# One more small read at the start of a kernel whose time is its transfers: 256 bytes of each partition's first row of strip 0, on ScalarE's DMA queue

## The chip, the cores and the metric

One core of one Trainium2 chip. HBM is the memory in which the input lies. A transfer (DMA) is issued by one of the compute engines on its queue and is carried out in packets by 16 transfer engines, which the text calls engines where packets are spoken of. The metric is the time of one execution on the device in microseconds (us), as the median of several runs; the span in a profile is the time from the first to the last instruction, and is some 1.7 us shorter. Ratios are the mean time of one kernel's fast runs over that of the other's of the same rounds, so not quite the ratio of the medians that are quoted.

## The reference

Four matrices of 4224 x 4224 fp32 numbers are summed up along both axes; of each result the diagonal is taken, and that is summed up once more.

```python
def reference(x):                       # x: (4, 4224, 4224) float32
    ps = np.cumsum(np.cumsum(x, axis=1), axis=2)
    diag = np.diagonal(ps, axis1=1, axis2=2)
    return np.cumsum(diag, axis=1).astype(np.float32)
```

Every number of the input counts, so 4 x 4224 x 4224 x 4 bytes = 285.5 MB have to be read once.

## The kernel before

The input is read in strips of 768 rows. A strip has 6 rows on each of the 128 partitions and is narrowed to bf16 by the load, which GpSimd issues. Three buffers hold strips. `head`, a corner of the last batch, stays fp32 and is loaded first, by SyncE; VectorE uses it at about 20 us.

```python
    head = last.tile([P, F, HC], FP32, name="head")            # P = 128, F = 3, HC = 384
    nc.sync.dma_start(out=head, in_=src[:, :, NH:N])
    # [cut: strip_tile]
    def load_rows(o, b, r0):
        f = o.shape[1]
        nc.gpsimd.dma_start(
            out=o, in_=x[b, r0 : r0 + f * P, :].rearrange("(p f) w -> p f w", f=f)
        )

    prefetched = []
    for i in range(NBUF):                                      # NBUF = 3
        t = strip_tile()
        load_rows(t, 0, i * F2 * P)                            # F2 = 6
        prefetched.append(t)
    # [cut: constants and masks]
    # for each strip, inside add_up:
            nc.vector.tensor_mul(out=mu, in0=block, in1=um)    # the diagonal block's masked part
            nc.vector.tensor_sub(out=block, in0=block, in1=mu)
            # [cut: TensorE sums columns; ScalarE (act_sum) and VectorE (row_sums) sum rows]
```

## Time and profile before

| | before |
|---|---|
| time, median of the first 3 runs | 667.07 us (667.06 to 667.53) |
| span of the profiled run | 665.4 us |
| read from HBM | 285.47 MB |
| first strip landed | 34.61 us |
| last load landed | 662.31 us |
| work after it | 3.1 us |

The page's tenths, queues, chain, waits and first windows are shown and read in the prediction. Besides these views I use the records of single DMA packets that the trace holds: start, duration, bytes and queue of each. Three rows of a strip arrive as one packet of 25,344 bytes written (50,688 read), which takes 1,886 ns; 16 of them on each of 16 engines are a strip, about 29.9 us. The records don't name the engine; where an engine is spoken of, I chained each packet to the one that ended just before it.

### The profile page before, as it was taken

Reading aid. Unit: us, or ns where it says so; the run is one execution under the profiler, and the core shown is the slowest. Engines: PE = TensorE matmul, PEld = TensorE weight load, DVE = VectorE, ACT = ScalarE, POOL = GpSimd, SP = SyncE. Lnnn points to the kernel's source line nnn. Section 1 sums busy time; section 2 is a strip of 40 time slices with the busy share of each in tenths; the row PEclk is TensorE's granted clock in tenths of the full one; section 3 lists DMA queues with packets and bytes.
Section 4 is the critical chain, followed back from the end, with each engine's and each line's share of the span. In section 5 each row is a group of like instructions: output and inputs, shape, how many; then the busy total and the mean of one; then the engine's idle time right before and its main releaser. Section 6 shows DMA issues by size and latency. Waiting matters only on the chain.

```text
span 665.4 us, 2461 instructions
## 1 busy us (share of the span) xinstructions
PE 201.7 (30%) x948; PEld 103.7 (16%) x948; DVE 326.4 (49%) x136; ACT 136.9 (21%) x222; POOL 31.8 (5%) x62
## 2 busy tenths in 40 slices
PE   0081423402007143140200623404032163250418
PEld 0040211201004021120100312202011031120103
DVE  3261625456906153454780524436388243352767
ACT  0001121406300103040630020304063002030434
POOL 6100000000000000000000000000000000001000
PEclk9995857656558585666755957666565586766758
DMA  9999999999999999999999999999999999999998
GB/s 206 219 219 219 219 219 215 212 210 218 219 218 219 219 220 218 218 213 212 216 218 218 217 219 219 218 219 211 215 216 219 219 214 220 216 219 216 214 208 162
DMA packets 7631, 143.25 MB, mean 215 GB/s; under 512 B 536, under 2 KB 1604, under 8 KB 2116
## 3 DMA queue, kind: packets, MB, share of 16 engines
q0 software_dynamic: 7152, 142.44, 99.9%
q1 hardware_dynamic: 468, 0.66, 0.3%
q8 instruction: 7, 0.11, 0.1%
q14 instruction: 4, 0.03, 0.0%
HBM read 285.47 MB, written 0.07 MB: 429 GB/s over the span
## 4 chain that ended last, share of the span: by engine, by line
another core or an unknown queue 44%; DVE 42%; DMA 11%; issue 1%; POOL 0%; PE 0%; DVEq 0%; POOLq 0%
DVE acc L246 27%; DMA strip<-in_x_dram 11%; DVE mu L333 7%; DVE strip L334 7%; DVE c L440 0%; POOL strip L411 0%; DVE rows L348 0%; PE d L226 0%; POOL strip L400 0%; DVE pu L246 0%; PE fin_e L226 0%; DVE c L266 0%; DVE pair L255 0%; PE carry_ps L226 0%
## 5 line engine op out<-in xcount | busy, mean ns | idle before, releaser
L226 PE MATMUL d<-strip,sel 128*33 128x384 bf16 (+1 forms) x603 | 140.7, 408 | 397.9 <-DMA strip<-in_x_dram 397.9
L241 ACT ACTIVATE dump<-strip 128x416 bf16<-128x416 bf16 (+6 forms) x110 | 125.1, 1138 | 520.5 <-DMA strip<-in_x_dram 517.8
L333 DVE TENSOR_TENSOR mu<-strip,um 128x4608 bf16<-128x4608 bf16 (+1 forms) x24 | 52.4, 2183 | 316.4 <-DMA strip<-in_x_dram 316.3
L246 DVE TENSOR_REDUCE acc<-strip 128x6 f32<-128x4608 bf16 (+6 forms) x23 | 196.0, 8523 | 0.8
L226 PEld LDWEIGHTS <-sel 128*33 128x33 bf16 (+1 forms) x849 | 94.9, 112 | 534.1 <-issue 495.9
L226 PE MATMUL d<-mu,sel 128*33 128x384 bf16 (+1 forms) x243 | 48.9, 353 | 45.4 <-DVE mu L333 45.4
L334 DVE TENSOR_TENSOR strip<-strip,mu 128x4608 bf16<-128x4608 bf16 (+1 forms) x24 | 52.4, 2183 | 1.0
L80 POOL DMA_DIRECT2D strip<-in_x_dram x24 | 16.5, 687 | 536.7 <-DVE acc L246 312.3
L241 ACT ACTIVATION_READ_ACCUMULATOR dump<-strip 128x1 f32 x110 | 20.5, 186 | 0.0
L226 PE MATMUL fold<-strip,ident_h 128*128 128x480 bf16 x8 | 3.4, 601 | 10.8 <-DMA strip<-in_x_dram 10.8
L96 DVE MEMSET um<- 128x6144 bf16 x1 | 5.2, 5178 | 1.2 <-issue 1.2
L216 DVE TENSOR_SCALAR steps<-steps 128x128 int32<-128x128 int32 x1 | 0.2, 227 | 11.0 <-POOL steps L215 11.0
L101 POOL TENSOR_SCALAR_AFFINE_SELECT um<-um 128x4608 bf16<-128x4608 bf16 (+1 forms) x2 | 5.2, 2614 | 4.0 <-DVE um L96 4.0
L226 PEld LDWEIGHTS <-ident_h 128*128 128x128 bf16 x21 | 2.2, 113 | 14.8 <-issue 13.8
L411 POOL DMA_DIRECT2D strip<-in_x_dram x5 | 2.7, 552 | 26.5 <-DMA strip<-in_x_dram 26.5
L226 PE MATMUL d<-ones_all,rows 128*33 128x128 f32 (+1 forms) x12 | 2.3, 347 | 5.4 <-DVE rows L348 5.4
L226 PE MATMUL fold_a<-strip,ident_h 128*128 128x512 bf16 x13 | 3.3, 380 | 0.3 <-DMA strip<-in_x_dram 0.3
L246 DVE TENSOR_REDUCE parts<-strip 128x3 f32<-128x3072 bf16 x1 | 3.4, 3352 | 0.0
L400 POOL DMA_DIRECT2D strip<-in_x_dram x2 | 1.4, 714 | 30.8 <-DVE acc L246 30.8
L226 PEld LDWEIGHTS d<-halves,rows 128*33 128x33 f32 (+1 forms) x24 | 2.5, 150 | 0.7 <-issue 0.5
L226 PE MATMUL d<-halves,rows 128*33 128x64 f32 (+1 forms) x24 | 2.6, 284 | 0.0
L348 DVE TENSOR_TENSOR rows<-acc 64x30 f32<-64x30 f32 (+2 forms) x12 | 2.1, 177 | 0.9
(80 smaller groups left out, 34.7 us busy)
## 6 DMA issues: line engine op xcount, KB each, us to landing
strip<-in_x_dram POOLq DMA_DIRECT2D x19, 6336.0 KB, 76.6
strip<-in_x_dram POOLq DMA_DIRECT2D x5, 3168.0 KB, 59.8
strip<-in_x_dram POOLq DMA_DIRECT2D x1, 1152.0 KB, 50.2
strip<-in_x_dram POOLq DMA_DIRECT2D x1, 768.0 KB, 53.3
strip<-in_x_dram POOLq DMA_DIRECT2D x3, 240.0 KB, 54.3
head<-in_x_dram SPq DMA_DIRECT2D x1, 576.0 KB, 4.0
strip<-in_x_dram POOLq DMA_DIRECT2D x1, 176.0 KB, 43.2
strip<-in_x_dram POOLq DMA_DIRECT2D x1, 64.0 KB, 28.6
```

What stands on the lines that cost most here:

```text
L80: nc.gpsimd.dma_start(out=o, in_=x[b, r0 : r0 + f * P, :].rearrange("(p f) w -> p f w", f=f))
L96: nc.vector.memset(um_all, 1.0)
L101: nc.gpsimd.affine_select(out=um, in_=um, compare_op=ALU.is_gt, fill=0.0, base=0, pattern=[[-1, f], [1, f * P]], channel_multiplier=-f,)
L216: nc.vector.tensor_single_scalar(out=steps, in_=steps, scalar=2, op=ALU.arith_shift_right)
L226: nc.tensor.matmul(o, lhsT=lhsT, rhs=rhs, start=start, stop=False, skip_group_check=True)
L241: nc.scalar.activation(out=dump[:, :w], in_=src, func=ACT.Copy, accum_out=acc)
L246: nc.vector.reduce_sum(out=acc, in_=src, axis=AX.X)
L333: nc.vector.tensor_mul(out=mu, in0=block, in1=um)
L334: nc.vector.tensor_sub(out=block, in0=block, in1=mu)
L348: nc.vector.tensor_add(out=o, in0=acc[..., 0], in1=acc[..., 1])
L400: nc.gpsimd.dma_start(out=part_a[:, :, c0:c1], in_=src_a[:, :, c0:c1])
L411: nc.gpsimd.dma_start(out=part_b[:, sb, c0:c1], in_=x[b, r0 : r0 + R, :NH].rearrange("r (k c) -> r k c", k=4)[:, :, c0:c1],)
```

## The change

ScalarE issues a read of 128 x 256 bytes, the first 64 numbers of each partition's first row of strip 0, into a tile that nothing uses. Its intent, as the words of it have it, is to touch that memory while the first load runs.

```diff
     head = last.tile([P, F, HC], FP32, name="head")
     nc.sync.dma_start(out=head, in_=src[:, :, NH:N])
+
+    touch = last.tile([P, 64], FP32, name="touch")
+    nc.scalar.dma_start(
+        out=touch, in_=x[0, : F2 * P, :].rearrange("(p f) w -> p f w", f=F2)[:, 0, :64]
+    )
```

## The prediction

> **What bounds the kernel now.** I read four views of the kernel before, in this order: the page (its tenths, DMA queues and HBM line), the chain that ended last, the waits, and the windows of the first microseconds.
>
> The page first, its engines, tenths, queues and bytes:
>
> ```profile
> PE 201.7 (30%) x948; PEld 103.7 (16%) x948; DVE 326.4 (49%) x136; ACT 136.9 (21%) x222; POOL 31.8 (5%) x62
> ...
> DMA  9999999999999999999999999999999999999998
> GB/s 206 219 219 219 219 219 215 212 210 218 219 218 219 219 220 218 218 213 212 216 218 218 217 219 219 218 219 211 215 216 219 219 214 220 216 219 216 214 208 162
> DMA packets 7631, 143.25 MB, mean 215 GB/s; under 512 B 536, under 2 KB 1604, under 8 KB 2116
> ## 3 DMA queue, kind: packets, MB, share of 16 engines
> q0 software_dynamic: 7152, 142.44, 99.9%
> q1 hardware_dynamic: 468, 0.66, 0.3%
> ...
> HBM read 285.47 MB, written 0.07 MB: 429 GB/s over the span
> ```
>
> No compute engine is busy for half of the span; the DMA engines are busy in every one of the 40 slices. The queue that GpSimd fills (q0, the strip loads, which narrow fp32 to bf16 on the way) alone accounts for 99.9% of the 16 engines' time. The bytes moved are counted as written (bf16), so 219 GB/s written stands for twice as much read: the HBM line gives 429 GB/s over the whole span, start and tail included.
>
> Next the chain that ended last, three pieces of it in order of time (start us, us, what):
>
> ```profile
> 1.33 33.28 DMA strip<-in_x_dram
> ...
> 619.08 43.23 DMA strip<-in_x_dram
> 662.33 0.40 DVE pair L255 x2
> ```
>
> The chain begins with the first strip's load, from 1.33 to 34.61 us, and its last load lands at 619.08 + 43.23 = 662.31 us; behind it there are only 665.4 - 662.3 = 3.1 us of work. In between the chain alternates between VectorE and pieces named "another core or an unknown queue" (44% on the page); those are the load waits once more, as the waits show:
>
> ```profile
> ACT dump L241 <- DMA strip<-in_x_dram: 517.8, 23, 62.4
> ...
> PE d L226 <- DMA strip<-in_x_dram: 397.9, 20, 34.7
> DVE mu L333 <- DMA strip<-in_x_dram: 316.3, 20, 19.8
> POOL strip L80 <- DVE acc L246: 312.3, 10, 32.2
> ```
>
> Every engine waits for strips, ScalarE longest: 62.4 us at one go, at the start. GpSimd in turn waits for a free buffer, but since three strips are in the buffers and two are queued while one is summed, the DMA tenths show no hole from that. So the end is set by the transfer engines' total work. Last, the windows of the start (columns: window, length, busy time of PE, PEld, DVE, ACT and POOL with counts, TensorE clock, DMA share, GB/s):
>
> ```profile
> 1.00:2.00 1.00, 0.00 (x0) 0.10 (x1) 0.08 (x2) 1.00 (x1) 0.67 (x1) 1.00 0.04 12
> 2.00:2.50 0.50, 0.00 (x0) 0.00 (x0) 0.13 (x1) 0.10 (x1) 0.50 (x2) 1.00 1.04 157
> 2.50:3.00 0.50, 0.00 (x0) 0.00 (x0) 0.50 (x1) 0.00 (x0) 0.50 (x2) 1.00 0.51 126
> ```
>
> The first packets run at about 1.9 us; until the strips begin at 3.8 to 4.5 us (the packet records, engine by engine) only the `head` tile that SyncE's queue reads is moving, and it doesn't fill the engines (0.51 between 2.5 and 3.0 us). Packets are entered at their starts in these short windows, so only the low shares mean something.
>
> **What the Trainium skill says.** Three places on its page "DMA: Bandwidth & Descriptors". Section "Issuing engines are not separate DMA queues": a DMA issued by ScalarE, SyncE or GpSimd ends up on the same 16 DMA engines and interleaves there. So the new read isn't free for being on ScalarE's queue. The trace agrees in kind: while the first result is stored, at 521 us, one 1,536-byte packet of SyncE's queue goes between two strip packets of an engine, and the spacing of those packets is 1,940 ns where strip packets alone follow each other every 1,866 ns. Section "Specifications": a fabric ceiling of 435 GB/s, and 512 bytes as the least transfer for line rate. For the ceiling the trace agrees: 285.47 MB between the first strip packet (3.8 us) and the last landing (662.3 us) is 433.5 GB/s. Whether a 256-byte packet costs more than its share is not shown before the change. Section "Why small descriptors are slow (HBM only)": a fixed overhead of about 3 cycles a packet, 11 cycles for 256 bytes where 8 carry data. The trace has nothing of that size that reads HBM; it has packets close by, used below.
>
> **The change part by part.** Nothing is removed, and nothing is moved: set side by side, the instruction lists of GpSimd, TensorE, VectorE and SyncE are the same up to buffer numbers and the number of the semaphore that `head` reports on. ScalarE gets one instruction more, a DMA issue ahead of its table load. Nothing reads the new tile, so no instruction waits for it.
>
> Step 1, the issue. SyncE's issue of `head` took 0.45 us. The same on ScalarE would move its table load from 0.81 to about 1.3 us, and its end from 2.1 to about 2.6 us. ScalarE's first sum starts at 64.54 us, after a wait of 62.45 us. On the path: 0.
>
> Step 2, the bytes. 128 rows x 256 bytes = 32.8 KB, against 285.47 MB: 0.011%. At 433.5 GB/s that is 0.076 us. This is the least that it can cost if the engines are full.
>
> Step 3, the packets. 128 rows over 16 engines are 8 packets on each, plus one that reports completion. On the page the hardware queue's 468 packets took 0.3% of 16 x 665.4 us, 32 us, or 68 ns each; the packet records give 65 ns for a `head` packet of 1,536 bytes, 11 ns for the one store packet of 128 bytes, and 9 ns for a completion behind `head`. A straight line through 128 bytes/11 ns and 1,536 bytes/65 ns gives 16 ns at 256 bytes. Estimate: 8 x 16 + 9 = 0.14 us an engine. If a small packet costs as much as a whole `head` packet: 8 x 65 + 9 = 0.53 us. If it costs double that again, 1.05 us.
>
> Step 4, what is hidden. ScalarE may issue at about 0.8 us, at the same moment as SyncE, so the new packets run beside those of `head`, between 1.9 and 4.5 us. The strip packets begin right behind an engine's last `head` packets in most cases, so there is a hole before them to fill on few engines; some of the 0.14 us may go into the 2.5 to 3.0 us hole. I count nothing as hidden, and put 0.05 us on top for a small penalty.
>
> Sum: 0 + 0.14 + 0.05 = about 0.2 us behind every later landing, and so behind the end: 667.07 + 0.2 = 667.3 us.
>
> **The rivals.**
>
> Rival A, fully hidden. The read goes into the engines' hole before the first strip packet, and the end doesn't move: 667.1 us. For it speaks the low share at 2.5 us; against it that the strips follow `head` closely. It differs from mine by less than the three runs before spread among themselves (0.47 us), so the time alone will hardly tell the two apart; only the landing of the first strip may.
>
> Rival B, packets that come late and cost a lot. If the strips' descriptors are on the engines first, the new packets take turns with 1,886-ns strip packets, one for one. Then the new read lands only 8 x 1.9 = 15 us after it starts; but a turn costs only the packet's own time. By the store at 521 us that is 1,940 - 1,866 = 74 ns a turn: 8 x 74 = 0.59 us, 667.7 us.
>
> Rival C, a warm start. The words "first row of strip 0" suggest that an early read opens a path or a row for the load after it. The first strip takes 33.28 us where one in the middle takes 29.9 (its landings at 125.27 and 155.16 us): 3.4 us more. Of those, 0.59 MB of `head` explain 1.4 us, and the rest is the time from issue to the first packet. Even if the touch took away all of that rest, 2.0 us, the time would be 665.1 us, 0.3% less. Against it: `head` is already an earlier read of HBM, the first strip packets last 1,885 to 2,229 ns against 1,886 later, which leaves at most 0.34 us on an engine, and what remains before them is GpSimd's issue, which the new read doesn't touch.
>
> Rival D, a new wait: the first use of ScalarE's DMA queue delays a shared resource, or the end of the program waits for one queue more. For the first nothing speaks in the profile; the second would be tenths, since the read lands hundreds of microseconds before. I give this 1 to 2 us at most: 668 to 669 us.
>
> **The range and the chances.** The middle is 667.3 us. From hidden (667.1) to interleaved (667.7) is 0.6 us; the runs before spread by 0.47 us, and single engines show pauses of about 0.9 us at chance places in the packet records, of which two on one engine would move the end by as much again. So 666.5 to 668.6 us. For more than 2% (13.3 us) slower, the engines would have to lose 13.3 x 433.5 GB/s = 5.8 MB worth of time, 176 times the new bytes. For more than 2% faster they would have to beat the ceiling: 285.47 MB / 435 GB/s = 656.3 us, plus 3.8 us of start, 3.1 us of tail and the 1.7 us between span and time is 664.9 us, 0.3% below the time before. Faster 0.01, same 0.98, slower 0.01.
>
> **What would show it.** In the changed kernel: the hardware queues hold 128 + 16 = 144 packets more (612 in all) and 0.03 MB more; the DMA tenths stay at 9; the read issued by ScalarE lands within 3 to 5 us if it runs beside `head`, and after about 15 us if rival B holds; the first strip lands about 0.2 us later than 34.6 us, the last load about as much later than 662.3 us; the tail stays 3.1 us. A first strip that lands more than 0.5 us earlier would show rival C. The prediction is wrong if strips in the middle, far from the new read, arrive at another spacing than 29.9 us, or if a wait for the new tile appears.

## The result, and the profile after

| | before | after |
|---|---|---|
| time, median of 6 runs each | 667.18 us (667.06 to 667.53) | 667.28 us (667.25 to 667.97) |
| ratio of the fast runs | | 1.0003 (95% interval 0.999 to 1.0016) |
| span of the profiled run | 665.4 us | 665.6 us |
| first strip landed | 34.61 us | 35.13 us |
| last load landed | 662.31 us | 662.46 us |

The page of the changed kernel, its DMA lines and queues:

```profile
DMA  9999999999999999999999999999999999999998
GB/s 208 219 219 218 219 216 216 209 216 218 219 218 219 219 218 219 213 213 215 218 218 219 216 219 219 218 216 216 212 219 215 219 217 220 218 216 218 216 207 162
...
q0 software_dynamic: 7152, 142.44, 99.9%
q1 hardware_dynamic: 468, 0.66, 0.3%
q8 instruction: 7, 0.11, 0.1%
q10 hardware_dynamic: 144, 0.03, 0.0%
q14 instruction: 4, 0.03, 0.0%
HBM read 285.51 MB, written 0.07 MB: 429 GB/s over the span
```

A queue for data has appeared beside q0 and q1: q10, with 128 + 16 packets. Its share rounds to nothing, and the other queues are as before (q8 and q14 were there too). Where the new instruction sits is seen in ScalarE's first instructions in order of time (start us, us, engine, line), and its landing in the view of the tile:

```profile
0.81 0.41 ACTq L76 DMA_DIRECT2D touch<-in_x_dram  x1
1.26 1.28 ACT L246 ACT_TABLE_LOAD   x1 [1.26 <-PEq L542]
```

```profile
L76 ACTq DMA_DIRECT2D touch<-in_x_dram x1: 413/413/413, 0.8 to 0.8; - x1
its engine sat idle before it (us, times) until:
who waited for it (us, times):
busy tenths in 40 slices 0000000000000000000000000000000000000000
DMA to landing us min/median/max: 2.7/2.7/2.7
```

The table load moves from 0.81 to 1.26 us, about as much as the issue takes. Below "who waited for it" there is no line: nobody does. The read lands 2.7 us after its issue, beside `head`. ScalarE's waits for strips, whose longest is the first, are nearly as they were (517.8 and 62.4 us before):

```profile
ACT dump L246 <- DMA strip<-in_x_dram: 517.5, 23, 62.5
```

The chain that ended last, at its two ends:

```profile
1.33 33.80 DMA strip<-in_x_dram
...
619.24 43.22 DMA strip<-in_x_dram
662.48 0.40 DVE pair L260 x2
```

The last load lands at 662.46 us, 0.15 us later than before, and what follows takes 3.1 us as before. But the first strip lands 0.52 us later, more than the time in the end. That asks for a look: it is not the size of the new read, as the experiments show.

### The profile page after: what moved, and what is told of

Same layout as the page of the kernel before. It is cut to its first block, busy times and chain, and to the rows that moved or that the text cites. A ratio compares the mean times of both kernels' runs of the same rounds, so it can differ in the third digit from the quotient of the medians.

```text
span 665.6 us, 2462 instructions
## 1 busy us (share of the span) xinstructions
PE 202.8 (30%) x948; PEld 103.6 (16%) x948; DVE 326.4 (49%) x136; ACT 136.9 (21%) x222; POOL 31.9 (5%) x62
## 4 chain that ended last, share of the span: by engine, by line
another core or an unknown queue 44%; DVE 42%; DMA 12%; issue 1%; POOL 0%; PE 0%; DVEq 0%; POOLq 0%
DVE acc L251 27%; DMA strip<-in_x_dram 12%; DVE mu L338 7%; DVE strip L339 7%; DVE c L445 0%; POOL strip L416 0%; DVE rows L353 0%; PE d L231 0%; POOL strip L405 0%; DVE pu L251 0%; PE fin_e L231 0%; DVE c L271 0%; DVE pair L260 0%; PE carry_ps L231 0%
```

## The experiments

Times of one kernel vary by more than the effect looked for, from 667.06 to 669.43 us for the kernel before over all rounds. So I give the lowest of a kernel's runs (I take it that disturbances only add, which is not shown) and, from the packet records, the median over the 16 engines of the start of the first strip packet. Runs with the kernel before of the same rounds beside them:

```
run              lowest  median us (fast runs)  before's lowest, median  start of strips us  last strip packet's end us
before (first)   667.06  667.18                 -                         4.17               662.33
after (first)    667.25  667.28                 667.06, 667.18            4.24               662.49
e1_many          668.40  668.56                 667.49, 668.46            5.47               663.88
e2_wide          668.15  668.25                 667.49, 668.46            5.06               663.34
e3_mid           669.51  670.23                 667.49, 668.46            4.13               664.70
e4_head_late     668.59  668.65                 667.49, 668.46            2.96               664.17
e5_before_again  667.19  667.56                 667.15, 668.04            4.11               663.13
e6_after_again   667.21  668.13                 667.15, 668.04            4.27               663.65
e7_other_rows    667.23  667.59                 667.15, 668.04            4.24               663.45
e8_sp_queue      667.25  667.71                 667.15, 668.04            4.27               662.47
e9_many64        669.10  669.59                 667.15, 667.96            5.01               664.30
e10_head_split   669.06  669.46                 667.15, 667.96            4.00               664.67
e11_after_third  667.16  667.42                 667.15, 667.96            4.17               662.61
```

All gave correct results, and by the rule of 2% each is "same". The runs e1 to e4 were on one chip, e5 to e11 on another.

The theory: the engines are full, all queues end on them, and each added packet costs its own time and nothing else. The rivals: it is hidden in the hole at the start; only bytes count; a packet costs much more, by itself or by its turn; reading strip 0's rows early warms something; ScalarE's queue has a price of its own.

### e1_many and e2_wide: twelve times the bytes, in small and in large packets

A tile that is used only at the end takes the read (the later code gets a view of it). The diffs of e1 to e3 are set against the changed kernel; none of the three holds the small read besides.

```diff
-    touch = last.tile([P, 64], FP32, name="touch")
+    c12_end = last.tile([P, 2, GW], FP32, name="c1211")
     nc.scalar.dma_start(
-        out=touch, in_=x[0, : F2 * P, :].rearrange("(p f) w -> p f w", f=F2)[:, 0, :64]
+        out=c12_end.rearrange("p a (k w) -> p (a k) w", w=64),
+        in_=x[0, : F2 * P, :].rearrange("(p f) w -> p f w", f=F2)[:, 0, : 792]
+        .rearrange("p (k w) -> p k w", w=66)[:, :, :64],          # e2_wide: [:, 0, :768] in one piece
     )
```

> The read at the start is made twelve times as large with the same 256-byte packets: 12 pieces of each partition's row, 1,536 packets, 96 on each transfer engine, 0.39 MB, into a buffer that is used only at the end. Theory (each packet costs its own time, 14 to 18 ns as the record of the changed kernel gives it, and nothing is hidden): 96 x 14 to 18 ns = 1.3 to 1.7 us, so 668.5 to 668.9 us against 667.2. Rival, bytes alone count: 0.39 MB / 433.5 GB/s = 0.9 us, 668.1 us. Rival, a small packet costs as much as one of head: 96 x 65 ns = 6.2 us, 673.4 us. Rival, hidden in the hole at the start: 667.2 us. If the strips' packets overtake it, its last packets take turns with them and it lands tens of microseconds later, without further cost.

> The same 0.39 MB as in the run before in one packet of 3,072 bytes for each partition: 128 packets, 8 on each engine. Theory of packets and of bytes alike: 8 x (3,072 bytes / 27.1 GB/s = 113 ns, plus some 5) = 0.94 us, 668.1 us. Against the run with 1,536 packets this isolates what the packets cost beyond their bytes: 0.4 to 0.8 us by the theory, 0 by the rival of bytes alone, 5 us by the rival of head-sized packets. Hidden in the hole: 667.2 us.

Measured, the queue lines and landings, first of e1_many and then of e2_wide:

```profile
q10 hardware_dynamic: 1552, 0.39, 0.3%
...
c<-in_x_dram ACTq DMA_DIRECT2D x1, 384.0 KB, 33.4
```

```profile
q10 hardware_dynamic: 144, 0.39, 0.2%
...
c<-in_x_dram ACTq DMA_DIRECT2D x1, 384.0 KB, 3.7
```

The strips start 1.34 us later than in the mean of the three traces with an undisturbed start (4.17, 4.13 and 4.11, so 4.14) with the small packets, and 0.92 us later with the large ones. The lowest times are 668.40 and 668.15 us, 1.3 and 1.0 us above 667.1, the lowest of before elsewhere; on this chip before's own lowest was 667.49 us, and its median lay between theirs, so by the ratios (1.0003 and 0.9998, intervals of a quarter of a per cent) the time alone settles nothing. The starts do: the large packets cost their bytes (0.92 against 0.94 us expected), nothing of them is hidden, and the small ones cost 0.42 us more before the strips begin. The rivals "hidden" and "as dear as a packet of head" (6.2 us) fall; "bytes alone" falls for small packets by that 0.42 us. The landing after 33.4 us shows that the strips overtook the tail of the small packets, which then took turns with them, as far as was expected. One packet record more shows how close the strips stand behind `head`: in the traces of before, of the changed kernel and of e2_wide, each of the 16 engines' first strip packets starts 5 or 6 ns after one of the 16 records of `head`'s completion.

### e3_mid: the small packets where all engines have strips queued

```diff
             add_up(strip, F2, s * F2 * P, acc6[:, s], um6)
+            if b == 0 and s == 1:
+                nc.scalar.dma_start(...)      # the read of e1_many; the one at the start is gone
```

> The read of 1,536 packets of 256 bytes, issued by ScalarE behind its sums of strip 1 (about 71 us), where every engine has strip packets queued; the read at the start is gone. Theory: it takes turns with strip packets, one for one, so it lands about 96 x 1.88 = 181 us after its issue, and each turn costs only the packet's own 14 to 18 ns: 1.3 to 1.7 us, 668.5 to 668.9 us. Rival B of the prediction (a turn costs 74 ns as at the store at 521 us): 96 x 74 = 7.1 us, 674.3 us. Rival, the whole read goes ahead of the strips: lands within 5 us.

The landing:

```profile
c<-in_x_dram ACTq DMA_DIRECT2D x1, 384.0 KB, 176.6
```

The theory's 181 us are nearly met: it took turns, one packet each. In 74 of 89 successive stretches of 1,893 ns exactly 16 of its packets start, one for each engine. The time is 1.0032 of before's (interval 1.0019 to 1.0045), 2.1 us or between 1.3 and 3.0, more than the 1.3 to 1.7 us of the theory and far below the 7.1 us of rival B. The packet records say why; they give the spacing of an engine's strip packets by what came between them (median of many, ns):

```
between two strip packets                     spacing   over none
nothing                                       1,867        -
one packet of 64 bytes (from e9_many64)       1,871        4
one packet of 256 bytes                       1,893       26
one completion of 4 bytes                     1,888       21
one packet of 1,536 bytes (head or a store)   1,940       73
```

A turn of a 256-byte packet costs 26 ns, not the 14 to 18 ns of a packet in a row of its kind, and not the 74 ns that I had read from the stores and taken for the price of any turn. 96 x 26 ns = 2.5 us, which agrees with the time. So theory and rival B were both off here, in the size of the term, not in the mechanism.

### e4_head_late: nothing in the hole

```diff
     head = last.tile([P, F, HC], FP32, name="head")
-    nc.sync.dma_start(out=head, in_=src[:, :, NH:N])
     # [cut]
     nc.vector.memset(um_all, 1.0)
+    nc.vector.memset(head[:, :, 0:1], 0.0)               # makes the load wait until about 8 us
+    nc.sync.dma_start(out=head, in_=src[:, :, NH:N])
```

> No added read; the load of head (0.59 MB, 1.4 us of all engines) waits until VectorE has finished the mask at about 8 us, so nothing moves in the hole before the first strip packet. If the strips' descriptors are ready early and head stands in their way, the first strip packets start about 1.4 us earlier (2.4 to 3 us) and the time stays at 667.2 us: then whatever runs before 3.8 us costs its full time. If the descriptors are not there before 3.8 us in any case, the first strip packets start at about 3.8 us, head's 24 packets an engine cost 24 x 61 ns = 1.5 us later on, and the time is 668.4 to 668.7 us: then head runs for free at the start today, and a small read beside it could be hidden. Head lands about 24 x 1.9 = 45 us after its issue; VectorE waits for it, with slack.

Two windows of its start, and the load's landing:

```profile
2.00:2.50 0.50, 0.00 (x0) 0.00 (x0) 0.13 (x1) 0.10 (x1) 0.50 (x2) 1.00 0.00 0
2.50:3.00 0.50, 0.00 (x0) 0.00 (x0) 0.50 (x1) 0.00 (x0) 0.50 (x2) 1.00 3.56 558
```

```profile
head<-in_x_dram SPq DMA_DIRECT2D x1, 576.0 KB, 50.8
```

Neither branch of the expectation holds whole. The strips' packets are ready early: they start at 2.96 us on the median, 1.2 us before the usual 4.14. So today they wait behind `head`, and what runs before them costs its time, which is the first branch. But the time seems not to have stayed: the lowest is 668.59 us against 667.1 to 667.5, though the ratio is 1.0004 (0.999 to 1.0018), so that the mean times show no difference. `head` now takes 24 turns an engine at 73 ns, 1.75 us, instead of the 1.2 us that it costs at the start, and strip packets that are longer than usual (40 above 1,900 ns, 0.8 us an engine together, against 0.1 us in the first trace of before) add some more. By the packets, reading `head` first is the cheaper place. Why the strips wait for `head` to finish at the start, where the packets of e3_mid take turns with them, is not shown.

### e5_before_again and e6_after_again: both kernels on one chip

No edit.

> The kernel before itself, as a control: its profile on the chip that runs the next three. Expected: time equal to that of the runs of before beside it within 0.1%; the 16 engines' first strip packets at 4.15 us on the mean (4.17 in the first trace, 4.14 in the run whose read came late, which starts as before), and 658.1 us from there to the last strip packet's end. If this chip is slower as the last one seemed to be (668.46 us), the second number is larger here and the first is not.

> The changed kernel as it is, on the same chip as the control. Theory: the first strip packets start 0.07 to 0.15 us later than in the control (4.25 against 4.15 to 4.17 us before), 658.1 us or the control's own number from there on; time 0.1 to 0.2 us over the control, which the spread of runs (0.5 us and more) may cover. Rival of the warm start: the stretch from first to last strip packet is shorter than in the control by more than 0.3 us.

The first and the last loads in the chains, first of before, then of after:

```profile
1.33 34.07 DMA strip<-in_x_dram
...
619.90 43.22 DMA strip<-in_x_dram
```

```profile
1.33 35.43 DMA strip<-in_x_dram
...
620.41 43.23 DMA strip<-in_x_dram
```

The control's first strip lands at 35.40 us, the changed kernel's at 36.76; in the first traces it was 34.61 and 35.13. By the median the engines start alike in each kernel (4.11 and 4.27 us), so it is single engines that are late: in the control the longest first strip packet takes 2,979 ns, in the changed kernel 3,298, where 1,886 is usual, and in the first trace of before none takes more than 2,229. A strip has landed when its slowest engine is done. This is the 0.52 us that the first trace after had too much (2,755 ns there). The start came 0.16 us later than in the control, at the edge of what was expected. My expectation for the rest (658.1 us from the mean first start to the last packet's end) failed: it was 659.0 us in the control, with 112 strip packets above 1,900 ns that cost 0.57 us an engine, against 12 and 0.14 us before. The stretch of the changed kernel is 659.36 us by the same measure, and not shorter than the control's, which speaks against a warm start. The two profiled runs were among the longer of their kernels, 667.94 and 668.47 us; their lowest times differ by 0.02 us.

### e7_other_rows: the same read from rows far away

```diff
-        out=touch, in_=x[0, : F2 * P, :]....
+        out=touch, in_=x[3, 2 * F2 * P : 3 * F2 * P, :]....
```

> The added read takes its 256 bytes from rows of another strip (batch 3, strip 2), which no load touches for 500 us; same size, queue and moment. Theory: as the changed kernel, first strip packets at about 4.25 us, same time within 0.1%. Rival of the warm start: whatever the read of strip 0's own rows gains is missing here, so strip 0 takes longer from its first packet to its last (29.88 us on most engines in both traces so far) or the time is above that of the changed kernel by more than 0.3 us.

Strips start at 4.24 us, the lowest time is 667.23 us, and 10 of the 16 engines need between 29.87 and 30.00 us for strip 0 (12 in the first trace of the changed kernel, 4 in the second). All within what the changed kernel itself shows; its first strip had one packet of 3,159 ns too. Which rows are read makes no difference that these runs could see, so the rival of a warm start has nothing left to stand on.

### e8_sp_queue: the same read on SyncE's queue

```diff
-    nc.scalar.dma_start(
+    nc.sync.dma_start(
```

> The same read issued by SyncE behind head instead of by ScalarE. Theory (all queues end on the same engines, and each packet costs its own time): head's packets first, then 8 of 14 to 18 ns on each engine, so the first strip packets start 0.1 to 0.15 us later than in the control; the read lands at 4.3 to 4.6 us instead of 3.2. Time as the changed kernel within 0.1%. Rival (the queue matters: a first use of ScalarE's queue costs something of its own): the start is at the control's time plus less than 0.05 us here, and later in the changed kernel.

```profile
1.33 33.36 DMA strip<-in_x_dram
...
619.20 43.22 DMA strip<-in_x_dram
```

The read runs behind `head`, from 3.94 to 4.46 us, its packets 14 ns apart where they follow each other directly; the strips start at 4.27 us, 0.13 us after 4.14; the lowest time is 667.25 us. The engines' starts and the time are as on ScalarE's queue, so the queue has no price of its own that these runs could see. Its first strip lands only 0.08 us after that of the first trace of before: here no first packet took more than 2,208 ns.

### e9_many64: more and smaller packets

The read of e1_many in 48 pieces of 64 bytes a row: `w=16` in the tile, pieces of 16 out of each 18 numbers in the source.

> The 0.39 MB of the large read at the start in pieces of 64 bytes: 48 a row, 6,144 packets, 384 on each engine. Theory (a packet has a floor of its own, some 7 to 11 ns as the 4- and 128-byte packets took 9 and 11): those that run before the strips' first packets (some 150 to 250 an engine) delay them by 1.5 to 2.5 us; the others take turns, one a turn of 1.88 us, so the read lands 250 to 450 us after its issue, at 15 to 30 ns a turn (the run in the middle gave about 25): 2 to 7 us more. Lowest time 670.5 to 676 us against the 667.1 of before. Rival of bytes alone: 668.1 us, as the wide read.

```profile
q10 hardware_dynamic: 6160, 0.39, 1.1%
...
c<-in_x_dram ACTq DMA_DIRECT2D x1, 384.0 KB, 475.9
```

The lowest time is 669.10 us, 2.0 us over 667.15 (ratio 1.0022, 1.0009 to 1.0036), and below the 670.5 us that I had put as the least: the turns were too dear in my estimate. 4,066 of the data and completion packets came after 5 us, 254 an engine; at 4 ns a turn (table above) that is 1.0 us, and the strips' start is 0.87 us late. Together 1.9 us. "Bytes alone" (668.1 us) falls. The page's 1.1% of the engines' time for this queue is 7.3 us an engine if taken literally, and the kernel loses 2.0: a packet in a turn is recorded with 24 ns and lengthens the spacing by 4, so its record overlaps with those of the strip packets, and the share of a queue isn't its cost.

### e10_head_split: can a second queue fill the hole?

```diff
-    nc.sync.dma_start(out=head, in_=src[:, :, NH:N])
+    nc.sync.dma_start(out=head[:, 0:1], in_=src[:, 0:1, NH:N])
+    nc.scalar.dma_start(out=head[:, 1:3], in_=src[:, 1:3, NH:N])
```

> No added read; head's three row groups are loaded by SyncE (one) and ScalarE (two), both at 0.8 us. If one queue's issue is what leaves the engines unfilled between 2.5 and 3 us, the first strip packets start 0.3 to 0.6 us earlier than 4.15 us and the lowest time falls from 667.1 to 666.6 us. If it is the wait for the first reads to come back, which both queues share, the start is 4.1 to 4.2 us and the time 667.1 us: then a second queue at the start can neither win nor cost more than its packets.

```profile
1.33 35.69 DMA strip<-in_x_dram
```

Slower: 669.06 to 669.80 us in all four runs, ratio 1.0018 (1.0004 to 1.0031). The median engine starts at 4.00 us, 0.14 us sooner, but three start only at 4.94, 5.61 and 6.19 us and stay behind, so that the first strip lands at 37.02 us and the last strip packet ends at 664.67 us. Why three engines get their strip packets late here is open; neither of my two branches foresaw it, and one trace can't tell.

### e11_after_third: the changed kernel once more

No edit.

> The changed kernel once more: lowest time of its runs 667.2 to 667.3 us against 667.05 to 667.2 us of before; first strip packets at 4.22 to 4.30 us on the mean, with the read landed by 3.2 us. If the first two traces' 0.1 us was chance, the start is at 4.10 to 4.18 us here.

The lowest time is 667.16 us, just under the range, and no different from before's 667.15; the start is 4.22 us on the mean (4.17 on the median), the read landed by 2.9 us. The starts of the changed kernel are so 4.24, 4.27 and 4.17 us (mean 4.23), against 4.17, 4.11 and 4.13 without a read at the start (mean 4.14): about 0.09 us, and the two groups just touch. e7_other_rows and e8_sp_queue, whose read is of the same size, started at 4.24 and 4.27 us and fall into the later group.

## Why the prediction was right

It was right in the whole: 667.28 us measured for 667.3, and "same", which had been given a chance of 0.98. That the two numbers meet so closely is luck: the interval of the ratio is 0.9 us wide to either side, the difference of the medians was 0.10 us where 0.2 had been forecast, and no run resolves so small a time. What the runs do test is the mechanism, with larger reads. Point by point:

- **The bound.** The transfer engines' work sets the time. e2_wide shows it: 0.39 MB more at the start push the strips back by 0.92 us, with 0.94 expected. The lowest time is 0.7 us above that of before beside it and 1.0 above that of the other rounds; the mean times show no difference. Nor is there idle time to fill: in the first trace of before, from 7 to 600 us, 16 packets or more are running at every moment when all queues are counted.
- **The ceiling.** The Trainium skill's page "DMA: Bandwidth & Descriptors", section "Specifications", gives the 435 GB/s for the side of SBUF, the on-chip memory, where the trace has 219 GB/s written. The 433.5 GB/s that the prediction sets beside it are read from HBM, so this is a likeness of numbers and no test of that ceiling, and the 664.9 us worked out from it are an estimate only.
- **Step 1, the issue: 0.** The table load moved by 0.45 us, and ScalarE still waited 62.5 us at one go for its first strip.
- **Step 2, the bytes: 0.076 us.** Only a lower bound, as said; e1_many, e3_mid and e9_many64 show that small packets cost more than their bytes.
- **Step 3, the packets: 0.14 us.** The 128 packets were recorded with 15 or 18 ns each, 2,196 ns in all, so 137 ns an engine, and 9 ns for a completion: 0.146 us. The line through two other packet sizes gave 16 ns. Back to back they follow each other every 14 ns.
- **Step 4, nothing hidden, and 0.05 us for a penalty.** About 0.09 us of later start were measured, with a spread of some 0.05, so neither part of it can be told apart; e4_head_late and e2_wide show that what runs before the strips is on the path. The prediction saw strips close behind `head` in most cases; the records show it on all 16 engines.
- **Rival A** (fully hidden) can't be excluded by the time for so small a read; the larger read and the starts speak against it.
- **Rival B** had the wrong price for a turn: 26 ns for 256 bytes, not 74. It didn't come to turns, since the read was over by 3.2 us, before the strips.
- **Rival C** (warm start) failed in e6_after_again and e7_other_rows. **Rival D** (a new wait) failed: nobody waits for the tile, the tail is 3.1 us, and e8_sp_queue is no different.

Two marks that I had named were poor. I expected the packets in the old hardware queue (612 in all); they came as a queue of their own, q10. And I named the first strip's landing as what would show 0.2 us: it is the landing of the slowest of 16 engines, and in three traces of the changed kernel it came at 35.13, 36.76 and 35.82 us, in two of before at 34.61 and 35.40. The range of 666.5 to 668.6 us holds the median, but 669.27 us in one of the 18 runs of the changed kernel was outside it, as were some runs of before: the spread of three runs was too narrow a guide.

The pauses of about 0.9 us that the prediction put "at chance places" have a cause in the same record. They are packets of the queue q8, which the page calls "instruction": seven of 16,384 bytes and 0.89 to 0.98 us each in the first trace of before (from 70, 204, 264, 376, 458, 544 and 627 us), and within 5 us of these times in every trace. Four of q14, of 8,192 bytes and 0.32 us, are the short ones. When they are counted, no pause is left between 7 and 600 us in that trace.

What is shown is that the effect is well below the noise, that the larger reads cost what their packets cost, and that no effect of the rows read or of the queue is to be seen at this size. The 0.09 us themselves rest on three starts against three, or five with the two other reads of this size.

## What to carry to other kernels

Where the transfer engines are full from end to end, price an added read by its packets and where they fall: in a row at their bytes plus a few ns, among large packets at a price a turn that grows with the packet. For pieces of 256 and 1,536 bytes a place in a row ahead of the big loads was cheaper (every 14 and 61 ns) than turns among them (26 and 73 ns a turn); for 64 bytes it was not (7 against 4 ns). When an effect is smaller than the spread of runs, enlarge it twelvefold and look at what the median engine does, not at the landing, which shows the slowest one. A longer first landing in one trace is no evidence until a second trace of the same kernel has it too.

## What the Trainium skill lacked or had wrong

- "DMA: Bandwidth & Descriptors", section "Queues, rings and completion order", says that an engine goes round-robin between its queues packet by packet; it has no price for a turn. Measured beside 1,867-ns strip packets: 4 ns for 64 bytes, 26 ns for 256, 73 ns for 1,536. It also says that a turn drains a packet of typically 9 to 17 descriptors; in e3_mid the small queue got one record of 256 bytes a turn (16 starts, one an engine, in 74 of 89 stretches of 1,893 ns). Whether a record of the trace is a packet or a descriptor in the page's sense is not shown.
- The same page, section "Specifications", gives 512 bytes as the least transfer for line rate. In a row, 256-byte pieces came every 14 ns, against 9.4 ns for their bytes at 27.1 GB/s an engine (433.5 / 16): below line rate, as it says, by a third. What that section lacks is the rate below 512 bytes; the overhead of 3 cycles in 11 that the prediction quotes from the same page would be 27% of the time, close to the third measured.
- I found no page that has the slow first packets of a large load: 2.2 to 3.3 us on one or a few engines where 1.886 us is usual, different from run to run. They set when the first strip lands, and I take them for part of the runs' spread; that was not tested.
